# One block layer with two attentions and 32 experts: seven block products in place of eight for half of each gate product's contraction, and experts taken from the four groups in turn

## The chip, the cores and the metric

The kernel runs on one core of one Trainium2 chip. The metric is the device time of one execution in microseconds (us); of several runs the median is given.

## What is computed

One transformer layer over 1024 tokens of width 1024, all in 32-bit floats, then a final norm. Cut to what matters here:

```
h = rmsnorm(x);  proj = h @ w_in            # 4288 columns
qa, ka, va, qi, ki, wi, qb, kvb, gb, gate_a, gate_b = split(proj)   # gate_a, gate_b: 1024 columns each
# branch a: each query keeps the 256 keys with the best index score (qi, ki, wi), then attends to them
score = sum_h wi[h] * relu(qi[h] . ki);  sel = top_k(score, 256)
# branch b: compressed, selected and windowed keys and values, with rope on the keys
merged = sigmoid(gate_a) * (o_a @ w_br_a) + sigmoid(gate_b) * (o_b @ w_br_b)
x = x + merged @ w_out
h = rmsnorm(x)
g = argmax(h @ w_group)                     # one of 4 groups for each token
top-2 of the 8 experts of that group, weighted;  x = x + sum_e w_e * (silu(gate) * up) @ w_down[e]
out = rmsnorm(x)
```

Each token belongs to one group only, so two experts of different groups never hold the same token.

## The kernel before

Every fp32 product runs as three TensorE matmuls: both factors are split into a rounded high part and the rest (h and l), and hh, hl and lh are summed in PSUM. A helper issues the three (the trace names them L238, L239 and L240 of `mm3`). The weights of `w_in` come by DMA as raw chunks of 256 columns; ScalarE (ACT) rounds the high part `wh` (L198) and GpSimd (POOL) subtracts it from the raw one for the low part `wl` (L199). `hTh` and `hTl` are the two parts of the transposed, normed tokens.

The work stands in this order. First the norm and the projections for the compressed branch. Then the query chunks; beside them the "units" of the index: TensorE multiplies the index keys `kist` with the queries (L609), ACT takes the relu (L611), VectorE (DVE) adds the weighted result into the score table `sc` (L615, the last with the row sums `st`). Then the K chunk (columns C_KV+256), 8 token tiles of 24 matmuls 128x256, with rope on POOL (L278 to L281) and transposes and sums into `kB` and `kA` (L667 to L685). Then the gates: 8 chunks (gate_a and gate_b, 2048 columns) of 96 matmuls 128x512, 4 results of 128 columns by 512 tokens each, each followed by a sigmoid on ACT (L860) and a store to `gscr`. Then the V chunk and attention, the merge, and the experts.

Beside the gate chunks DVE looks for each query's 256th best score: 7 rounds (`NCOUNT`) of 6 counts `sc >= th` (L774, widths 384 to 1024), each round but the last followed by some 17 small instructions on 128x6 that narrow the threshold (L781 to L806). Then it writes `okr` (L811), which says whether every query's count was near enough; TensorE transposes it (L813) for the one-row test of a fallback. After that DVE writes the mask `qbias` (L827 to L837).

```
for c in range(8):
    hi, lo = next_chunk()
    for m in range(2):
        for n in range(2):
            ps = ps1.tile([P, 512], F32, name="pj", bufs=2)
            for k in range(KD):
                mm3(ps, hi[:, k, ...m...], lo[:, k, ...m...], hTh[:, k, ...n...], hTl[:, k, ...n...], k == 0, k == KD - 1)
            prefetch()
            ...
            act.activation(gt, ps, AF.Sigmoid)
```

The instructions of the engines are put in an order ahead of the run by a scheduler that knows durations and priorities; each engine then works its list strictly in that order and waits where an operand is not there. So a DVE instruction that is late holds everything behind it on DVE, and a matmul that waits for it holds all matmuls behind it.

The experts run one after the other, 8 of one group and then 8 of the next. For each, weights are streamed and split (`gh`, L1472, `gl`, L1473), tokens are gathered (`xg`, L1453) and transposed (L1463), 96 matmuls make `u` (L238 to L240), silu (L1486, L1495), then `down` (yp, L1504) of the expert before. The weighted result `y` (ACT L1506, DVE L1508) is added to the table `acc` in device memory by an indirect DMA on POOL's queue (`spread`, L1512), each behind the one before. The results of the last two experts stay in SBUF (`keep`, L1625 to L1627, `NL` = 2) and are added to the 8 token tiles of `acc`, read back as `ck` (L1564), by one-hot matmuls (L1643) and a DVE sum (L1644). Then the final norm: L1581 to L1598, and the scaling, on ACT (L1604), POOL (L1583) or DVE (L1608: one instruction 128x1024 with both factors).

Of the kernel before, what the change touches and what calls it, by code (L numbers as in the profile page):

```python
# [20 lines left out]
P = 128  # L21
# [45 lines left out]
ORDER = (2, 3, 7, 6, 5, 1, 4, 0)  # L67

# [33 lines left out]
def emit(tc, A):  # L102
# [107 lines left out]


    chunks = [((C_KV, 256), (C_KI, 32)), ((C_QI, 256), (C_WI, 8), (C_GB, 24))]
# [8 lines left out]
    def prefetch(n=1):  # L221

        if not coming and chunks:
            coming.append(load_chunk(*chunks.pop(0)))
# [70 lines left out]
    def make_list(pl, ps, nm, as_f32=False):  # L295
# [14 lines left out]
        dve.tensor_scalar(i0, f[:, :NXG], -1.0, float(S - 1), op0=OP.add, op1=OP.min)  # L310
# [262 lines left out]
    def index_units(ip):  # L573
# [27 lines left out]
        for t in range(2, NT):  # L601
# [3 lines left out]
            for h in range(8):  # L605
# [11 lines left out]
                if h == 7:  # L617

                    jk = ip.tile([P, 1024], F32, name="jks", bufs=1)
                    act.activation(jk[:, :n], acc, AF.Square, accum_out=st2[:, t - 2:t - 1])  # L620
# [15 lines left out]
    sc = scq.tile([P, 33 * P], F32, name="sc")  # L636
    with ExitStack() as pk:
# [49 lines left out]
        def roped(ps, t):  # L687
            qn = kq.tile([P, 4, 64], F32, name="qn", bufs=4)
            (dve.tensor_copy if t in QND else act.copy)(qn, ps[:, 0:256].rearrange("p (h d) -> p h d", h=4))
            qr = kq.tile([P, 4, 64], F32, name="qr", bufs=4)  # L690
# [3 lines left out]
        def step(t):  # L694
            for _ in range(RATE[t % 2]):
                next(units, None)

        for br, c0 in ((1, C_QB), (0, C_QA)):
            for c in range(2):
                hi, lo = next_chunk()  # L700
                for t in range(NT):
# [10 lines left out]
                    qstack(srcs, t, c)  # L712
        for _ in units:
            pass
        pu.close()

        kp = mkpool(pm, "kp", side="left", reuse_waits="tile")
        kB = [kp.tile([P, 2, 2, S], F32R, name=f"kB{x}") for x in range(2)]
        hi, lo = next_chunk()
        for t in range(NT):  # L720
            ps = project(t, hi, lo, 256)
            _, kr = roped(ps, t)
            if t % 4 == 0:

                ka = kq.tile([P, 4, 64], F32, name="ka")
                cs, sn = (x[:, t:t + 4, None].to_broadcast([P, 4, 2, 32]) for x in (cos, sin))
                ra, rb = (kq.tile([P, 4, 2, 32], F32, name=n, bufs=1) for n in ("ra4_32", "rb4_32"))
                pool.tensor_tensor(ra, kaN[:, t:t + 4], cs, op=OP.mult)
                pool.tensor_tensor(rb, kaN[:, t:t + 4], sn, op=OP.mult)
                kav = ka.rearrange("p t (a b) -> p t a b", a=2)  # L730
                dve.tensor_tensor(kav[:, :, 0], ra[:, :, 0], rb[:, :, 1], op=OP.subtract)
                dve.tensor_tensor(kav[:, :, 1], ra[:, :, 1], rb[:, :, 0], op=OP.add)
            if t % 2:
                late.append(lambda ka=ka, t=t: kapost(ka, t))
            later[1].append(lambda kr=kr, t=t: kpost(kr, t))
        flush()

    with ExitStack() as pk:
        kq = mkpool(pk, "gq", bufs=2, side="left", reuse_waits="tile")
# [5 lines left out]
        with ExitStack() as pt:  # L745
# [93 lines left out]
            with tc.If(fv > 0):  # L839
                for t in range(2, NT):  # L840
# [7 lines left out]
                    dve.tensor_scalar(bias[:, soff[t]:soff[t] + n], y[:, :n], -2.5e38, NEG, op0=OP.is_gt, op1=OP.mult)  # L848

        for c in range(8):  # L850
            hi, lo = next_chunk()
            for m in range(2):
                for n in range(2):
                    ps = ps1.tile([P, 512], F32, name="pj", bufs=2)
                    for k in range(KD):
                        mm3(ps, hi[:, k, m * P:(m + 1) * P], lo[:, k, m * P:(m + 1) * P],
# [881 lines left out]
```

## Time and profile before

| what | value |
|---|---|
| median of 3 runs | 1379.64 us (1377.6 to 1382.06) |
| the profiled execution | 1379.86 us |
| its span | 1378.2 us |
| mean granted TensorE clock | 0.984 |
| busy: PE, DVE, ACT, POOL | 1314.9, 918.9, 699.8, 473.2 us |

Times in the trace count from the start of the span; the profiled execution takes 1.66 us more than its span. PE is TensorE's matmul, DVE VectorE, ACT ScalarE, POOL GpSimd. A row of the timeline gives the start, how long the instruction took, engine, line, what it writes and reads, and in brackets how long the engine stood idle before it and what ended that. Matmuls are pipelined: a row's duration is longer than the distance to the next row, and the distance is what counts.

### The profile page before, as it was taken

The page shows a single profiled execution, that of the slowest core. Times are in us where ns is not written, and L with a number is a line of the kernel's source. Part 1 is how long each engine was busy: PE and PEld are TensorE (multiplying, and loading weights), DVE is VectorE, ACT ScalarE, POOL GpSimd, SP SyncE. Part 2 cuts the span into 40 slices and gives each one's busy share as a digit, 9 for nine tenths or more (in the row PEclk, how much of TensorE's full clock was granted, in tenths as well). Part 3 has the DMA queues.
Part 4 walks back from the last instruction along what each step waited for, and adds up shares of the span by engine and source line. Part 5 has one row for each costly group of instructions (what it writes and reads, how often), then busy time and mean ns, then how long its engine had stood idle before and what let it go on. Part 6 is the DMA issues. An engine that isn't in the chain of part 4 may idle for free. (4 is left out here: it accounts for less than half of the span.)

```text
span 1378.2 us, 21458 instructions
## 1 busy us (share of the span) xinstructions
PE 1314.9 (95%) x7135; PEld 1021.3 (74%) x7135; DVE 918.9 (67%) x2285; ACT 699.8 (51%) x1458; POOL 473.2 (34%) x564
## 2 busy tenths in 40 slices
PE   7999999999999999999999999999699999998993
PEld 6999999988888766666667688877566667665652
DVE  7866877689600588777677686566776767655745
ACT  5615676622211576666676742222366657545544
POOL 0316777722212474444454300000123223223114
PEclk9999999999999999999999999999899999999997
DMA  5513543223333120101110384685799997899866
GB/s 190 124 28 95 158 128 112 70 89 96 93 99 115 31 78 16 31 16 32 46 47 16 107 225 128 205 304 184 240 321 299 323 336 250 260 301 321 298 194 244
DMA packets 127733, 215.34 MB, mean 156 GB/s; under 512 B 24042, under 2 KB 62994, under 8 KB 127618
## 3 DMA queue, kind: packets, MB, share of 16 engines
q1 hardware_dynamic: 111842, 174.53, 38.4%
q0 software_dynamic: 13680, 34.04, 9.2%
q10 hardware_dynamic: 2096, 5.36, 1.0%
q8 instruction: 57, 0.93, 0.3%
q14 instruction: 58, 0.48, 0.1%
HBM read 180.38 MB, written 49.28 MB: 167 GB/s over the span
## 5 line engine op out<-in xcount | busy, mean ns | idle before, releaser
L995 ACT ACTIVATE pg<-pg,nm 128x512 f32<-128x512 f32 (+7 forms) x192 | 139.0, 726 | 49.0 <-DVE nm L994 35.2
L238 PE MATMUL pj<-wh,hTh 128*128 128x288 f32 (+1 forms) x512 | 152.8, 299 | 2.4 <-ACT hTh L421 1.4
L240 PE MATMUL pj<-wh,hTl 128*128 128x288 f32 (+1 forms) x512 | 151.4, 296 | 2.3 <-DVE hTl L422 2.3
L239 PE MATMUL pj<-wl,hTh 128*128 128x288 f32 (+1 forms) x512 | 150.9, 295 | 0.8 <-DVE wl L199 0.8
L199 POOL TENSOR_TENSOR wl<-wr,wh 128x512 fp32r<-128x512 f32 (+1 forms) x60 | 81.5, 1368 | 201.3 <-ACT wh L198 192.2
L1013 PEld LDWEIGHTS tr<-ident,pg 128*128 128x128 f32 x784 | 87.9, 141 | 50.6 <-issue 24.3
L239 PE MATMUL u<-gl,xh 128*128 128x512 f32 x256 | 109.7, 429 | 3.6 <-DVE gl L1473 3.6
L1013 PE MATMUL tr<-ident,pg 128*128 128x128 f32 x784 | 111.1, 277 | 0.0
L238 PE MATMUL u<-gh,xh 128*128 128x512 f32 x256 | 107.2, 419 | 0.7 <-ACT gh L1472 0.7
L240 PE MATMUL u<-gh,xl 128*128 128x512 f32 x256 | 102.2, 399 | 0.0
L238 PE MATMUL pj<-hTh,wh 128*128 128x512 f32 x256 | 101.2, 395 | 0.0
L240 PE MATMUL pj<-hTh,wl 128*128 128x512 f32 x256 | 101.1, 395 | 0.0
L1473 DVE TENSOR_TENSOR gl<-cr,gh 128x1024 fp32r<-128x1024 f32 x68 | 81.7, 1221 | 29.0 <-ACT gh L1472 16.7
L239 PE MATMUL pj<-hTl,wh 128*128 128x512 f32 x256 | 100.8, 394 | 0.0
L1512 POOL DMA_INDIRECT acc<-y,lis x30 | 53.8, 1792 | 136.8 <-ACT y L1506 77.0
L238 PEld LDWEIGHTS pj<-wh,hTh 128*128 128x128 f32 x512 | 97.1, 190 | 4.2 <-ACT hTh L421 2.0
L240 PEld LDWEIGHTS pj<-wh,hTl 128*128 128x128 f32 x512 | 96.8, 189 | 3.8 <-DVE hTl L422 3.1
L239 PEld LDWEIGHTS pj<-wl,hTh 128*128 128x128 f32 x512 | 97.1, 190 | 1.9 <-DVE wl L199 1.0
L916 DVE COPY pth<-tr 128x512 f32<-128x512 f32 (+1 forms) x102 | 69.9, 686 | 38.7 <-PE tr L1013 32.5
L1473 DVE TENSOR_TENSOR gl<-ck,gh 128x1024 fp32r<-128x1024 f32 x55 | 66.6, 1222 | 32.9 <-PE u L239 22.0
L975 PE MATMUL s<-kB,q 128*128 128x384 f32 (+3 forms) x384 | 82.8, 344 | 3.1 <-DVE nm L994 3.0
L916 ACT COPY pth<-tr 128x512 f32<-128x512 f32 (+1 forms) x102 | 58.8, 578 | 46.7 <-PE tr L1013 25.2
(590 smaller groups left out, 3394.5 us busy)
## 6 DMA issues: line engine op xcount, KB each, us to landing
cr<-in_w_gate_up SPq DMA_DIRECT2D x68, 512.0 KB
ck<-in_w_gate_up SPq DMA_DIRECT2D x55, 512.0 KB
cr<-in_w_down SPq DMA_DIRECT2D x32, 512.0 KB
ck<-in_w_down SPq DMA_DIRECT2D x30, 512.0 KB
wr<-in_w_in SPq DMA_DIRECT2D x52, 256.0 KB
qscr<-qTs SPq DMA_DIRECT2D x96, 128.0 KB
q<-qscr POOLq DMA_DIRECT2D x24, 512.0 KB, 3.6
xt<-in_x SPq DMA_DIRECT2D x16, 512.0 KB
```

The lines of the kernel that those rows point to most:

```text
L199: eng.tensor_tensor(lo[:, k:k + 2, w], raw[:, :, w], f32(hi[:, k:k + 2, w]), op=OP.subtract))
L238: pe.matmul(ps, lh, rh, start=first, stop=False)
L239: pe.matmul(ps, lh, rl, start=False, stop=False)
L240: pe.matmul(ps, ll, rh, start=False, stop=last)
L916: return h[:n], (act.copy if EV[ev[0] % len(EV)] else dve.tensor_copy)(h[:n], tr[:n])
L975: mm_, mm = mm, pe.matmul(s2s[x][:, c:c + w_], q()[:, place(h + x)], kk[:, y, j0 * P + c:j0 * P + c + w_], start=y == 0, stop=y == 1)
L995: act.activation(pg, pg, AF.Exp, bias=nm[:, y:y + 1], scale=-1.0, accum_out=sm_[:, y:y + 1])
L1013: pe.transpose(tr[:, hh * P:(hh + 1) * P], pgs[4 * g + hh][:, c:c + P], ident)
L1473: dve.tensor_tensor(gl, w, f32(gh), op=OP.subtract)
L1512: pool.indirect_dma_start(out=acc[:], out_offset=bass.IndirectOffsetOnAxis(ap=idx, axis=0), in_=y, in_offset=None, compute_op=OP.add, boun ...
```

## The change

In each of the gate chunks 1 to 7 (chunk 0 stays as it was) the first half of the contraction, k tiles 0 to 3, is taken as a product of two by two blocks (2 blocks of 128 columns and 2 pairs of k tiles, against 2 pairs of k tiles and 2 blocks of 512 tokens) in seven block products in the place of eight. The second half is done as before. A chunk has 90 matmuls then, not 96. Four of the seven products take sums of token blocks (`sumh`, `suml`, made once in `token_sums`) and three of weight blocks (`sh`, `sl`, made for every chunk by POOL and ACT). The results of several products are shared: they are copied or added in PSUM by ACT (L835, L845) and DVE (L836, L844, L849, L855, L860), five DVE sums of 128x512 in each chunk. The K chunk moves from ahead of the gates to behind them; the transposes for `kA` that went with it move ahead into the last query chunk.

Of the experts one of each group is taken in turn (`EORD`). A spread waits for the fourth before it only, no longer for the three between. The read-back waits for the last four spreads. `keep` of expert 30 runs inside expert 31. In the final norm DVE's scaling reads the gains from PSUM (two matmuls put them there) in two halves.

```diff
+EORD = tuple(8 * g + i for i in range(8) for g in range(4))
...
+    def load_gates(cols):
...
+        def split(h, l, src):
+            act.activation(h, src, AF.Copy)
+            pool.tensor_tensor(l, src, f32(h), op=OP.subtract)
...
+            if k == 2:
...
+                pool.tensor_tensor(f, q[:, :, m[0]], q[:, :, m[1]], op=OP.subtract)
+                split(hi[:, 0:2, m[1]], lo[:, 0:2, m[1]], f)
+                pool.tensor_tensor(f, q[:, :, m[1]], r[:, :, m[1]], op=OP.add)
+                split(sh[:, 0], sl[:, 0], f)
+                pool.tensor_tensor(f, f, q[:, :, m[0]], op=OP.subtract)
+                split(sh[:, 1], sl[:, 1], f)
+                pool.tensor_tensor(f, r[:, :, m[0]], f, op=OP.subtract)
+                split(sh[:, 2], sl[:, 2], f)
...
+    chunks += [((C_GA + 256 * c, 256),) for c in range(8)]
     chunks += [((C_KV + 256, 128), (C_KV + 512, 128))]
-    chunks += [((C_GA + 256 * c, 256),) for c in range(8)]
...
+    def token_sums(pl):
...
+        with tc.high_priority():
+            for k in range(2):
+                for c in range(0, 512, 256):
+                    f = [pl.tile([P, 256], F32, name=f"tf{j}", bufs=1) for j in range(4)]
...
+                        dve.tensor_tensor(f[j], f32(hTh[:, kk + k, at]), f32(hTl[:, kk + k, at]), op=OP.add)
+                    for j, o, x, y in ((0, 0, 1, 0), (1, 1, 2, 1), (2, 2, 2, 0), (3, 3, 3, 2)):
+                        dve.tensor_tensor(f[o], f[x], f[y], op=OP.subtract)
+                        act.activation(th_[:, j, k, cs], f[o], AF.Copy)
+                        dve.tensor_tensor(tl_[:, j, k, cs], f[o], f32(th_[:, j, k, cs]), op=OP.subtract)
...
+            a, b = (ps1.tile([P, 1024], F32, name="s2", bufs=2) for _ in range(2))
+            a, y, z, d = a[:, :512], a[:, 512:], b[:, :512], b[:, 512:]
+            u2, u3 = (kist2[:, j * 512:(j + 1) * 512] for j in range(2))
+            v = ps1.tile([P, 512], F32, name="pj", bufs=2)
+            part(a, w(0, 0), x(0, 0), True, True)
+            part(y, S2, T2, True, True)
+            with tc.high_priority():
+                act.activation(u2, a, AF.Copy)
+                dve.tensor_tensor(u2, y, u2, op=OP.add)
+            part(a, w(2, 0), x(2, 0), False, False)
+            rest(a, 0, 0, False)
+            gate_group(0, 0, a, c)
+            prefetch()
+            part(y, S3, T3, True, True)
+            part(z, S1, T1, True, True)
+            with tc.high_priority():
+                dve.tensor_tensor(u3, y, u2, op=OP.add)
+                act.activation(v, z, AF.Copy)
+            part(d, w(2, 1), T4, True, False)
+            rest(d, 1, 0, False)
+            with tc.high_priority():
+                dve.tensor_tensor(d, d, u3, op=OP.add)
+            gate_group(1, 0, d, c)
+            prefetch()
+            part(z, S4, x(2, 1), False, False)
+            rest(z, 0, 1, False)
+            with tc.high_priority():
+                dve.tensor_tensor(z, z, u2, op=OP.add)
+            gate_group(0, 1, z, c)
+            prefetch()
+            rest(v, 1, 1, False)
+            with tc.high_priority():
+                dve.tensor_tensor(v, v, u3, op=OP.add)
+            gate_group(1, 1, v, c)
+            prefetch()
...
-                        pin(dve.scalar_tensor_tensor(xt, xt, r1, gfin, op0=OP.mult, op1=OP.mult))
+                        for n in range(2):
+                            ns = slice(n * 512, (n + 1) * 512)
+                            pin(dve.scalar_tensor_tensor(xt[:, ns], xt[:, ns], r1, gains[n], op0=OP.mult, op1=OP.mult))
...
-            xts = load_acc()
+            xts = load_acc(spreads[-4:])
...
-                    spread(down(late_[2], dn, lwt[:, col[e]]), lidx[:, col[e]])
+                    i = spread(down(late_[2], dn, lwt[:, col[e]]), lidx[:, col[e]])
+                    if len(spreads) >= 4:
+
+                        for j in spreads[-3:]:
+                            tc.declare_no_dep(i.ins, j.ins, reason="tokens of different groups")
+                        behind(i, spreads[-4], True)
+                    spreads.append(i)
```

`part` issues 6 matmuls (2 k tiles, three each) and `rest` 12. The matmuls of chunks 1 to 7 are all named L807 in the changed kernel, those of chunk 0 L281 to L283, the counts L927, `okr` L964 and its transpose L966.

How the list of TensorE moves at the transpose of `okr`. In the kernel before, all 192 matmuls of the K chunk and 386 of the gates stand ahead of it (`pj` is a gate's result):

```order
L238 MATMUL pj<-hTh,wh 128x512
L239 MATMUL pj<-hTl,wh 128x512
L813 MATMUL tr<-ident,okr 1x128
L240 MATMUL pj<-hTh,wl 128x512
L238 MATMUL pj<-hTh,wh 128x512
```

In the changed one (`s_4745` holds a and y, `s_4746` z and d of chunk 3):

```order
L807 MATMUL s_4745<-hTl,wh 128x512
L807 MATMUL s_4745<-hTh,wl 128x512
L807 MATMUL s_4746<-sumh,wh 128x512
L807 MATMUL s_4746<-suml,wh 128x512
L807 MATMUL s_4746<-sumh,wl 128x512
L966 MATMUL tr<-ident,okr 1x128
L807 MATMUL s_4746<-sumh,wh 128x512
L807 MATMUL s_4746<-suml,wh 128x512
```

Now 315 of the gates' matmuls and none of the K chunk stand ahead of it, and 411 of the gates' behind it.

The list of DVE between the third and the fourth round of counts. Before, only the threshold's small instructions stand there (the first six of them):

```order
L774 TENSOR_SCALAR y,cnt<-sc,th 128x1024
L781 TENSOR_SCALAR mk<-cnt 128x6
L788 TENSOR_SCALAR t_3693<-cnt 128x6
L782 COPY_PREDICATED lo__3688<-mk,th 128x6
L783 COPY_PREDICATED cl<-mk,cnt 128x6
L784 TENSOR_SCALAR mk<-cnt 128x6
```

In the changed kernel three sums of chunk 1 stand among them (`kist` is u3, `s_4456` d, `pj` v):

```order
L927 TENSOR_SCALAR y,cnt<-sc,th 128x1024
L934 TENSOR_SCALAR mk<-cnt 128x6
L941 TENSOR_SCALAR t_3550<-cnt 128x6
L935 COPY_PREDICATED lo__3545<-mk,th 128x6
L936 COPY_PREDICATED cl<-mk,cnt 128x6
L937 TENSOR_SCALAR mk<-cnt 128x6
L938 COPY_PREDICATED hi__3546<-mk,th 128x6
L844 TENSOR_TENSOR kist<-s_4455,kist 128x512
L939 COPY_PREDICATED ch<-mk,cnt 128x6
L849 TENSOR_TENSOR s_4456<-s_4456,kist 128x512
L860 TENSOR_TENSOR pj<-pj,kist 128x512
```

Eleven such sums (five each of chunks 1 and 2, one of chunk 3) stand on DVE between the first count and `okr`, and TensorE's list waits for them: the next block product into the same PSUM tile, or the next chunk's, has one of these sums, or the sigmoid behind it, as its condition. Five more stand among the instructions that write the mask.

On ACT, near the end of the experts, the last of `down` stands behind the silu (`sg`) before, and ahead of it now:

```order
L1486 ACTIVATE sg<-u 128x256
L1506 ACTIVATE y<-yp,lws 128x512
L1472 ACTIVATE gh<-cr 128x1024 x3
L1495 ACTIVATE aT<-at 128x256
L1472 ACTIVATE gh<-cr 128x1024
```

```order
L1662 ACTIVATE y<-yp,lws 128x512
L1628 ACTIVATE gh<-cr 128x1024
L1642 ACTIVATE sg<-u 128x256
L1628 ACTIVATE gh<-cr 128x1024 x2
L1651 ACTIVATE aT<-at 128x256
```

Both pieces stand near the end of the expert stage. TensorE's `down` moves with it, ahead of the last 5 matmuls of the expert that runs beside it.

## Rows read from the trace of the kernel before

**Rows 1.** Page, busy time and share of the span by engine, instructions.

```profile
PE 1314.9 (95%) x7135; PEld 1021.3 (74%) x7135; DVE 918.9 (67%) x2285; ACT 699.8 (51%) x1458; POOL 473.2 (34%) x564
```

**Rows 2.** Windows: busy us (instructions) of PE, PEld, DVE, ACT, POOL, clock, DMA share.

```profile
300.00:350.00 50.00, 50.00 (x218) 40.44 (x217) 47.30 (x163) 9.95 (x19) 10.35 (x9) 1.00 0.29 90
...
400.00:450.00 50.00, 50.00 (x265) 42.68 (x264) 0.85 (x2) 7.90 (x15) 9.88 (x10) 1.00 0.35 106
```

**Rows 3.** Timeline of PE: first K matmul, okr's transpose, V's first matmul.

```profile
231.91 0.36 PE L238 MATMUL pj<-wh,hTh 128*128 128x256 f32 x1
...
349.70 0.27 PE L813 MATMUL tr<-ident,okr 128*1 128x128 f32 x1
...
438.36 0.28 PE L238 MATMUL pj<-wh,hTh 128*128 128x256 f32 x1
```

**Rows 4.** Timeline of DVE: last scores, starts of rounds 1 to 3, okr, mask's end.

```profile
248.10 1.28 DVE L615 SCALAR_TENSOR_TENSOR sc<-s,raw,sc 128x1024 f32<-128x1024 f32 x1 [0.50 <-ACT s L611]
...
284.67 0.61 DVE L774 TENSOR_SCALAR_CACHE_REDUCE y<-sc,th 128x384 bf16<-128x384 f32 x1
...
293.16 0.61 DVE L774 TENSOR_SCALAR_CACHE_REDUCE y<-sc,th 128x384 bf16<-128x384 f32 x1
...
301.04 0.61 DVE L774 TENSOR_SCALAR_CACHE_REDUCE y<-sc,th 128x384 bf16<-128x384 f32 x1
...
343.71 0.14 DVE L811 TENSOR_REDUCE okr<-mk 128x1 f32<-128x6 f32 x1
...
367.34 1.22 DVE L837 TENSOR_SCALAR qbias<-y 128x896 bf16<-128x896 f32 x2
```

**Rows 5.** Groups of DVE by shape, 231 to 281 us: the work on kA.

```profile
L684 DVE SCALAR_TENSOR_TENSOR kA<-tr,kA 64x128 fp32r<-64x128 f32 x8 | 2.3, 288 | 4.2 <-ACT kA L682 4.1
L685 DVE CAST kA<-kA 64x256 fp32r<-64x256 f32 x4 | 1.8, 442 | 0.1
```

**Rows 6.** Timeline of DVE: sums of two SBUF operands, 341 to 343 us.

```profile
341.83 0.55 DVE L828 TENSOR_TENSOR y<-y,sc 128x384 f32<-128x384 f32 x1
342.30 0.15 DVE L809 SCALAR_TENSOR_TENSOR mk<-cnt,t 128x6 f32<-128x6 f32 x1
...
342.64 0.68 DVE L828 TENSOR_TENSOR y<-y,sc 128x512 f32<-128x512 f32 x1
```

**Rows 7.** Timeline: a small DVE instruction of the search, and POOL beside it.

```profile
283.28 1.27 DVE L794 TENSOR_TENSOR t<-sd,tkc 128x6 f32<-128x6 f32 x1
...
283.22 2.58 POOL L199 TENSOR_TENSOR wl<-wr,wh 128x512 fp32r<-128x512 f32 x2 [4.61 <-ACT wh L198]
```

**Rows 8.** Chain that ended last, pieces in time order: start, us, what.

```profile
1346.07 0.70 DVE ck L1644
...
1361.90 3.14 DVE ck L1608
...
1366.35 1.28 DVE ck L1608
```

**Rows 9.** Timeline of ACT: the sigmoid of a gate result.

```profile
271.76 0.60 ACT L860 ACTIVATE gt<-pj 128x512 f32<-128x512 f32 x1
```

**Rows 10.** Waits of PE, 1290 to 1345 us: total, times, longest.

```profile
PE yp L1504 <- ACT y L1506: 1.1, 1, 1.1
PE yp L1625 <- ACT y L1506: 1.1, 1, 1.1
```

**Rows 11.** Timeline: the last two spreads, the last y, the last kept result.

```profile
1329.61 1.56 POOL L1512 DMA_INDIRECT acc<-y,lis  x1 [8.52 <-DVE gl L1473]
1336.42 1.56 POOL L1512 DMA_INDIRECT acc<-y,lis  x1 [5.25 <-DVE ck L1627]
...
1332.15 0.68 ACT L1506 ACTIVATE y<-yp,lws 128x512 f32<-128x512 f32 x1
...
1342.39 0.75 DVE L1627 SCALAR_TENSOR_TENSOR ck<-yp,lws,ck 128x512 fp32r<-128x512 f32 x1 [0.97 <-ACT ck L1626]
```

**Rows 12.** Windows, 24 to 32 us (columns as in Rows 2).

```profile
24.00:32.00 8.00, 6.28 (x28) 5.30 (x28) 7.48 (x20) 5.45 (x15) 0.00 (x0) 0.59 0.23 67
```

More of the change, by code (lines that the diff above doesn't have):

```diff
@@ L715, in emit @@
         pu.close()
[L717 to L735, printed above, removed]
@@ L736, in emit, with gate_group, part @@
-        flush()
-    with ExitStack() as pk:
-        kq = mkpool(pk, "gq", bufs=2, side="left", reuse_waits="tile")
+        pg0 = ExitStack()
+        gq.append(mkpool(pg0, "g0", bufs=2, side="left", reuse_waits="tile"))
+        def gate_group(m, n, ps, c):
+            gt = gq[0].tile([P, 512], F32, name="gt")
+            act.activation(gt, ps, AF.Sigmoid)
+            sp.dma_start(gscr[2 * c + m, :, n * 512:(n + 1) * 512], gt)
+        def part(ps, a, b, first, last):
+            (ah, al), (bh, bl) = a, b
+            for k in range(2):
+                for x, y in ((ah, bh), (ah, bl), (al, bh)):
+                    pe.matmul(ps, x[:, k], y[:, k], start=first and k == 0 and y is bh and x is ah,
+                              stop=last and k == 1 and x is al, skip_group_check=True)
@@ new lines, in emit, with first_gates @@
+        token_sums(gq[0])
+        first_ = next_chunk()
+        def first_gates(m):
+            hi, lo = first_
+            for n in range(2):
+                ps = ps1.tile([P, 512], F32, name="pj", bufs=2)
+                for k in range(KD):
+                    mm3(ps, hi[:, k, m * P:(m + 1) * P], lo[:, k, m * P:(m + 1) * P],
+                        hTh[:, k, n * 512:(n + 1) * 512], hTl[:, k, n * 512:(n + 1) * 512], k == 0, k == KD - 1)
+                if m:
+                    prefetch(2)
+                gate_group(m, n, ps, 0)
+                if not m:
+                    todo = later[0] + late
+                    later[:] = later[1], []
+                    late.clear()
+                    for f_ in todo:
+                        f_()
@@ L742, in emit @@
+        first_gates(0)
+        pg0.close()
+    pg_ = ExitStack()
+    gq[:] = [mkpool(pg_, "gq", bufs=2, side="left", reuse_waits="tile")]
+    first_gates(1)
+    with pg_:
         bias = small.tile([P, 33 * P], BF, name="qbias")
@@ L871, in emit @@
     flush()
+    pk.close()
     p1.close()
@@ L1569, in final @@
             pin = tc.keep_in_program_order
+            gains = [gfin[:, n * 512:(n + 1) * 512] for n in range(2)]
             s1s, q1s, z1s, r1s = {}, {}, {}, {}
@@ L1578, in sums @@
                 if add:
-                    add(t, xts[t])
+                    i = add(t, xts[t])
+                    if t == 3:
+                        for n in range(2):
+                            gp = psf.tile([P, 512], F32, name="yp", bufs=2)
+                            behind(pe.matmul(gp, ident, gains[n], start=True, stop=True), i)
+                            gains[n] = gp
                 jk = ft.tile([P, D], F32, name="y", bufs=NY)
@@ L1686, in between @@
                 turn_next(e + 1)
+            elif c >= 2 and e + 1 == NE:
+                keep((c - 2,))
         for c in range(4):
```

123 lines of the change are left out of this document (92 added, 31 removed).

## The prediction

> **What bounds the kernel now.** I read the page first: TensorE is busy for 1314.9 of 1378.2 us [rows 1], so it idles for 63 us in all, and what moves the time is what shortens or delays its own list. The windows come next [rows 2]. From 300 to 350 us PE is busy for every microsecond at clock 1.00, with 217 matmuls of 128x512 (0.23 us each), and VectorE has 47.30 us of work; from 400 to 450 PE is as full and DVE has 0.85. DVE is thus nearly full beside the first half of the gates and idle beside the second, and this costs nothing today, for one reason: the only matmul that waits for the counting is the transpose of `okr`, issued at 349.70 [rows 3], and DVE writes `okr` from 343.71 on [rows 4]. The slack is nearly 6 us. The end of the kernel is the other place without cover: there the chain that ended last runs from a spread over the read-back to DVE's sums and scaling.
>
> **The change part by part.**
>
> *Products.* Seven chunks with 90 matmuls in place of 96 are 42 fewer; 50.00 us hold 217 [rows 2], so 0.23 each: −9.7 us of PE.
>
> *The K chunk behind the gates.* Its 192 matmuls cost PE the same there. What goes is cover. Today PE starts it at 231.91 and reaches `okr`'s transpose 117.8 us later [rows 3]. In the changed list 315 gate matmuls, 14 index matmuls and 11 small transposes stand between the same point and that transpose: 329 × 0.23 = 75.7, and 11 × 0.15 = 1.7 (an estimate: a row of such a transpose reads 0.27, and rows overlap). PE would be there at 309.3, 40 us sooner.
>
> *DVE until `okr`.* Today the last scores end at 249.4, counting starts at 284.67, and `okr` is there at 343.85 [rows 4], 59.2 us later. Changed:
> - The work on `kA` now stands ahead of the last scores: 8 × 0.288 + 4 × 0.442 = 4.1 us [rows 5]. The scores end at 253.5.
> - 48 token sums of 128x256. No row has that size with two SBUF operands; 384 took 0.55 and 512 took 0.68 [rows 6], so 256 takes about 0.42; the next row starts 0.08 before an end (341.83 and 0.55, then 342.30): 48 × 0.34 = 16.3. The search's 22 preparing instructions lie between: 2.5 at 0.11 each, an estimate below the 0.15 that such a row takes [rows 6]. Counting starts at 272.3.
> - From the first count to `okr` 59.2, as today. Six rounds of 7.88 when undisturbed (293.16 to 301.04 [rows 4]) are 47.3, and the last one's counts and the tail about 8.1 (an estimate: 17 small instructions fewer than a round's 7.88 leave 5.2, and 2.9 go to the tail), so 3.8 of it are delays. They are small instructions beside a POOL one: 1.27 in place of 0.15, until the first half of POOL's 2.58 was over [rows 7]. POOL's work for a chunk goes from 2048 elements a partition to 3840, nearly double: 3.8 more.
> - 11 gate sums of 128x512. The nearest row, one operand in PSUM, took 0.70 [rows 8], some 0.60 from start to start: 6.6.
>
> Sum: 272.3 + 59.2 + 3.8 + 6.6 = 341.9. **TensorE waits about 33 us in place of none**, and not in one piece. Its first wait is for the token sums: chunk 1's z stands behind 102 gate matmuls, so PE is there near 261, while the sums end near 272 and ACT and POOL still have to split `sh`. The others are for the sums u2 and u3 and for sigmoids behind z, each of which has a round of counts in front of it.
>
> The Trainium skill's page "SBUF — State Buffer" (section "SBUF: two separate sides") says that GpSimd and a VectorE instruction with two SBUF inputs lock each other out for a whole instruction. Rows 7 agree, with 1.27 us. By that rule the 48 token sums too would stand in line with whatever POOL does beside them, which makes the sum above longer, not shorter.
>
> *After `okr`.* DVE writes the mask, 343.85 to 368.5 today, 24.7 us [rows 4], with five gate sums (3.0) among it; the last of these lets PE go on, 69 matmuls (15.9 us) behind the transpose: 27.7 − 15.9 = 11.8, less the two mask writes behind that sum (1.2): 10 us. Then DVE is free from 400 us on [rows 2], and a chain is left at three chunk ends: product, DVE sum 0.70, sigmoid 0.60, next chunk's product into the same PSUM tile [rows 8, 9]: 1.3 and the handovers, 5 in all.
>
> Gates and K together: −9.7 + 33 + 10 + 5 = **+38 us**. Bounds: if the scores end as today and no instruction is delayed at all, the wait is 33 − 4.1 − 7.6 = 21 and the total +26; if a sum of two PSUM operands, which no row has, takes a pass for each, 11 × 0.6 more, +45. I take the middle: the sum with one PSUM operand is the nearest row.
>
> The Trainium skill's page "VectorE: DVE Perf Modes" (section "Why PSUM operands drop a tier") states that VectorE has one read port to PSUM. An estimate by it would be two passes for such a sum; no row here shows one.
>
> *Copies, weight sums, DMA.* ACT has 9.95 and POOL 10.35 us of work in 50 [rows 2]: two copies a chunk on the one and twice the work on the other hide there, and the bytes are the same. Zero.
>
> *Experts and end.* Bytes and matmuls of the 32 experts stay. Two waits of PE for ACT's `y`, 1.1 each [rows 10], go, since `y` stands ahead of the silu. The last spread is issued at 1336.42, 6.8 behind the one before, though its `y` was ready at 1332.83 [rows 11]; unhooked, it lands some 4 us sooner. Next in line is the last kept result, ready at 1343.14 [rows 11], and two waits sooner at 1341: so the first sum moves from 1346.07 [rows 8] to about 1341.2, −4.9. L1608 of 3.14 us becomes two halves of the undisturbed 1.28 [rows 8]: −1.8. Two fp32 matmuls for the gains: +0.9 at most. **−6 us**; bounds −2 (landings side by side stretch each other) and −9.
>
> **Sum:** 1379.9 + 38 − 6 = 1412 us; the profiled run lies 0.2 above the median, so this stands against that as well. A change below 0.3% (4 us) can't be told from none by a measurement of this kernel.
>
> **Rivals.**
> - *Light tie, 1400 us.* The scores end as today and nothing is delayed: 1379.9 + 26 − 6. For it: whole rounds have no late row (293.16 to 301.04). Against it: POOL's longer work. 0.16.
> - *The other side, 1364 us.* DVE answers every gate sum before PE asks, because the sums have priority over the counts: 1379.9 − 9.7 − 6. It decides at the transpose of `okr`: DVE has to be there by 309, and by about 315 for the whole kernel to break even (6 us of wait, 10 behind it). Rounds and tail alone are 55.4, so counting would have to begin near 254, which leaves no room for the token sums. Against it: the list has them in front. 0.07.
> - *Heavy tie, 1425 us.* PSUM sums cost double (+7), and the gaps cost clock: between short idle times early on, 6.28 of 8.00 us busy, the granted clock was 0.59, near the 1.2 GHz level [rows 12]; a gate matmul at that level takes 0.23 more, and 25 of them are +6. For it: the 43 us of waiting come in several pieces. Against it: while DVE is the bound, a slow PE is partly hidden. 0.15.
> - *The expert part gives nothing,* 1418: a case inside the forecast's range.
>
> **How the numbers follow.** The forecast has 0.62, the light tie 0.16, the heavy one 0.15, the other side 0.07. The range leaves out the other side and the outer parts of the two ties: 1394 to 1431. Slower by over 0.3%: 0.90; faster: 0.07; within 0.3%: 0.03, as little lies between the light tie and the other side.
>
> **What would show it.** In the profile after: PE idle for some 45 us between 260 and 440, released by DVE L844 and L836 and by ACT's sigmoid; `okr` near 342 and its transpose right behind; V's first matmul near 476 in place of 438.36 [rows 3]; 128x512 sums of about 0.7; the first sum of the tail right behind the last kept result. I would be wrong if `okr` came before 325, if PE had no long waits ahead of it, or if the gate sums were far from 0.7.

## The result and the profile after

The changed kernel takes 1429.68 us (median of 4 runs, 1427.22 to 1431.28) against 1378.95 us for the kernel before (4 runs): ratio 1.0356, 95% interval 1.0333 to 1.038. It is slower by 50.7 us. The forecast was 1412 us with a range of 1394 to 1431: the direction and the range held, the range by 1.3 us at its upper end, and the middle lay 17.7 us too low.

The page of the changed kernel, engine by engine: busy time, share of the span, instructions. The next line is the granted clock of TensorE in 40 slices.

```profile
PE 1332.3 (93%) x7097; PEld 1028.5 (72%) x7097; DVE 967.4 (68%) x2370; ACT 721.3 (50%) x1516; POOL 509.7 (36%) x620
...
PEclk8999999799899999999999999999979999999998
```

Against [rows 1] PE has 38 matmuls fewer (42 fewer in the gates, 4 more for the gains of the final norm) and is busy 17.4 us longer, and the span grew by 51.3 us. So PE both waits more and is slower while it works. The windows of the gate stage of the changed kernel show both (columns as in [rows 2]: busy us of PE, PEld, DVE, ACT and POOL with their instructions, clock, DMA share, GB/s):

```profile
260.00:300.00 40.00, 25.06 (x93) 18.89 (x91) 39.21 (x125) 14.00 (x31) 18.07 (x22) 0.83 0.23 66
300.00:350.00 50.00, 40.85 (x154) 31.87 (x155) 47.58 (x146) 12.89 (x27) 19.27 (x23) 0.90 0.24 74
350.00:400.00 50.00, 40.35 (x149) 30.86 (x147) 27.18 (x50) 8.97 (x20) 13.91 (x16) 0.86 0.21 64
400.00:450.00 50.00, 44.62 (x183) 35.42 (x184) 7.74 (x12) 15.19 (x32) 21.73 (x25) 0.96 0.28 85
```

From 300 to 350 us PE was full at clock 1.00 before [rows 2]; now it is busy 40.85 of 50 us and starts 154 matmuls and transposes where it started 218. The granted clock is 0.83 to 0.90 as long as DVE is busy with the search and the mask, and even from 400 on, where DVE has 7.74 us of work in 50, PE is not full.

Where PE waited in the changed kernel, from 225 to 500 us (who waits, for whom: us in total, times, longest); it is the view's whole answer:

```profile
PE s L807 <- ACT gt L799: 18.1, 7, 5.0
PE s L807 <- DVE kist L844: 10.3, 3, 5.2
PE s L807 <- ACT sh L225: 9.1, 1, 9.1
PE s L807 <- DVE kist L836: 1.6, 1, 1.6
PE s L807 <- DVE sc L658: 1.3, 1, 1.3
PE s L652 <- DVE sc L658: 1.3, 2, 0.9
PE tr L741 <- DVE qTs L721: 0.9, 2, 0.6
```

`gt` is the sigmoid (ACT), `kist` the sums u2 and u3 (DVE), `sh` the rounded weight sums. The kernel before has no such wait in its gates.

**Where 51.3 us of span come from.** I cut each span at two places that both kernels have: attention's first matmul (461.19 us before, 516.43 after) and the transpose of the experts' first gathered tokens (1001.65 and 1057.63). Up to attention the change adds 55.2 us, between the two places 0.7, and behind the second it saves 4.6 (376.51 to 371.91). The 55.2 are, by the list of PE's starts: 42 matmuls fewer, −9.7; 47.1 in 23 gaps (a gap is here and below a step of over 0.5 us from the start of a 128x512 matmul to the next start, less 0.23); 77 matmuls of 128x512 that are some 0.43 us from the next in place of 0.23, +14.9; the rest, some 3, was not followed further. Of the 23 gaps 15 are waits, 44.3 us. The other 8, 2.9 us, are no idle time: they are the first steps behind a wait where the granted clock was already at 0.50, 0.56 to 0.59 us in place of the 0.34 that such a step takes at 1.00. So the lower clock makes 14.9 + 2.9 = 17.8 us, and the waits 44.3.

### The profile page after: what moved, and what is told of

It is laid out like the page before. It is cut to its first block, busy times and chain, and to the rows that moved or that the text cites. A ratio compares the mean times of both kernels' runs of the same rounds, so it can differ in the third digit from the quotient of the medians.

```text
span 1429.5 us, 21637 instructions
## 1 busy us (share of the span) xinstructions
PE 1332.3 (93%) x7097; PEld 1028.5 (72%) x7097; DVE 967.4 (68%) x2370; ACT 721.3 (50%) x1516; POOL 509.7 (36%) x620
## 4 chain that ended last, share of the span: by engine, by line
PE 78%; DVE 11%; DMA 4%; ACT 3%; issue 3%; DVEq 0%; POOL 0%; ACTq 0%; POOLq 0%
PE av L1079 7%; PE yp L1660 7%; PE s L1131 7%; PE tr L1169 7%; PE s L807 6%; PE pj L283 4%; PE pj L281 4%; PE pj L282 4%; PE ps L281 4%; PE u L282 4%; PE ps L283 4%; PE ps L282 4%; PE u L281 4%; PE u L283 3%; DVE y L927 2%
## 5 line engine op out<-in xcount | busy, mean ns | idle before, releaser
L283 PE MATMUL pj<-wh,hTl 128*128 128x288 f32 (+1 forms) x512 | 152.0, 297 | 2.7 <-DVE hTl L465 2.7
L281 PE MATMUL pj<-wh,hTh 128*128 128x288 f32 (+1 forms) x512 | 152.9, 299 | 1.6 <-ACT hTh L464 1.4
L1668 POOL DMA_INDIRECT acc<-y,lis x30 | 51.3, 1709 | 186.7 <-ACT y L1662 161.7
L282 PE MATMUL u<-gl,xh 128*128 128x512 f32 x256 | 113.4, 443 | 1.8 <-DVE gl L1629 1.5
L281 PE MATMUL u<-gh,xh 128*128 128x512 f32 x256 | 105.5, 412 | 3.1 <-ACT gh L1628 3.1
L283 PE MATMUL u<-gh,xl 128*128 128x512 f32 x256 | 102.1, 399 | 0.0
L283 PEld LDWEIGHTS pj<-wh,hTl 128*128 128x128 f32 x512 | 97.2, 190 | 3.8 <-DVE hTl L465 3.5
L281 PEld LDWEIGHTS pj<-wh,hTh 128*128 128x128 f32 x512 | 97.6, 191 | 2.9 <-ACT hTh L464 1.8
L1629 DVE TENSOR_TENSOR gl<-ck,gh 128x1024 fp32r<-128x1024 f32 x55 | 66.8, 1225 | 37.0 <-PE u L282 17.7
L1628 ACT ACTIVATE gh<-cr 128x1024 fp32r<-128x1024 f32 x68 | 70.7, 1058 | 34.4 <-DMA cr<-in_w_gate_up 26.4
L201 POOL TENSOR_TENSOR wl<-wr,wh 128x576 fp32r<-128x576 f32 (+1 forms) x32 | 44.8, 1408 | 108.7 <-ACT wh L200 99.2
L1150 DVE CUSTOM_DVE_ANT_0 pg<-s,causal 128x256 f32<-128x256 f32 (+7 forms) x112 | 65.0, 616 | 7.6 <-PE s L1131 7.2
L1628 ACT ACTIVATE gh<-ck 128x1024 fp32r<-128x1024 f32 x55 | 58.2, 1060 | 23.2 <-DMA ck<-in_w_gate_up 11.0
```

Of the source, the lines that this page charges most:

```text
L281: pe.matmul(ps, lh, rh, start=first, stop=False)
L282: pe.matmul(ps, lh, rl, start=False, stop=False)
L283: pe.matmul(ps, ll, rh, start=False, stop=last)
L1628: act.activation(gh, w, AF.Copy)
L1629: dve.tensor_tensor(gl, w, f32(gh), op=OP.subtract)
```

## The experiments

Eight kernels, each timed beside the kernel before. Their ratios are to that kernel on the same chip.

### One part alone: the experts and the end

The front is as before, with K ahead of the gates and eight products everywhere; the turns of the groups, the spreads, `keep` inside expert 31 and the new end stay.

Edit, against the kernel before:

```diff
+EORD = tuple(8 * g + i for i in range(8) for g in range(4))
...
+                    if len(spreads) >= 4:
+
+                        for j in spreads[-3:]:
+                            tc.declare_no_dep(i.ins, j.ins, reason="tokens of different groups")
+                        behind(i, spreads[-4], True)
...
-            xts = load_acc()
+            xts = load_acc(spreads[-4:])
```

> The kernel before with the second part of the change alone: experts of the four groups in turn, spreads that wait for the fourth before, keep split, gains of the final norm in PSUM; gates and K chunk as before. My theory: this part is worth what the trace of the changed kernel shows from the first transposed token of the experts to the end of the span, 371.9 us against 376.6: about -4.7, so 1374 us (1372 to 1377), and V's first matmul stays near 438. Rival: the expert part shares in the loss (its spreads side by side slow the weight streams), the gates lose less than 55: then this one is no faster than before, 1379 or more.

Measured: 1373.88 us against 1380.86, ratio 0.9945 (0.9927 to 0.9963). The stretch from the experts' first transpose to the end is 371.0 us, 5.5 shorter than before, and the attention starts at 462.04, 0.9 later than before. So this part gains, the whole loss is in the front, and **this kernel beats both**: by 0.55% against the kernel before, and the interval leaves 1 out.

### All eight products, K still behind the gates

Edit, against the changed kernel:

```diff
-            coming.append(load_gates(cols) if C_GA < cols[0][0] < C_END else load_chunk(cols, eng))
+            coming.append(load_gates(cols) if C_GA + 256 * 8 <= cols[0][0] < C_END else load_chunk(cols, eng))
...
-        token_sums(gq[0])
...
+                    for k in range(KD):
+                        mm3(ps, hi[:, k, m * P:(m + 1) * P], lo[:, k, m * P:(m + 1) * P],
+                            hTh[:, k, n * 512:(n + 1) * 512], hTl[:, k, n * 512:(n + 1) * 512], k == 0, k == KD - 1)
```

> The changed kernel with eight products in every gate chunk, as before; the K chunk stays behind the gates, the experts in turn. My theory: the loss of 55 us ahead of attention is that of the seven-product scheme in chunks 1 to 7 (waits of 47 us, 77 matmuls at half clock), and the moved K chunk costs next to nothing: 1374 to 1379 us, no wait of PE over 3 us between 260 and 440, okr near 320 with its transpose when PE gets there. Rival: the moved K chunk, which takes away PE's cover of 27 us, makes PE wait at okr whatever the gates do: 1390 us or more.

Measured: 1383.03 us against 1380.86, ratio 1.001 (0.9995 to 1.0026), above what I expected. The attention starts at 468.52, 6.5 later than in the kernel above, from which it differs by K's place and what moved with it (the transposes for `kA` and the sizes of a few buffers). Its waits in the gate stage, in the same view:

```profile
PE pj L281 <- ACT gt L800: 2.4, 1, 2.4
PE s L652 <- DVE sc L658: 1.3, 2, 0.9
PE tr L742 <- DVE qTs L722: 0.9, 2, 0.6
```

All three lie near 245 to 252 us, where the last query chunk's index units end. In the kernel before, K's matmuls (231.91 to 258.85) stand at this place and cover them; 10 half-rate matmuls behind them add 2. `okr` is there at 316.83 and nothing waits for it. So with eight products the move of K costs about 6.5 us, through small waits at the seam and not through `okr`. Seven products with K still ahead of the gates were not run; what K's place costs together with them is open.

### DVE set free

The search rounds and the mask's making are left out (the counts and the mask are constants); all else of the change stays.

Edit, against the changed kernel:

```diff
-            for it in range(NCOUNT):
-                count()
...
+            dve.memset(cnt, TOPK - 2.0)
...
+            dve.memset(bias, 0.0)
```

> The changed kernel with the search left out: no rounds of counts, and the mask of the 256 best keys is a constant zero. Token sums, gate sums and all matmuls stay. My theory as on record (DVE's counts stand in front of the gate sums) says that the waits ahead of okr and beside the mask go, and what is left is the wait for the token sums (about 11 us) and a chain at the end of each chunk, DVE sum and sigmoid into the next chunk's tile (2.4 us each at six or seven ends): some 28 us in place of 47, fewer matmuls at half clock, 1398 to 1406 us. Rival: the seven-product scheme has these waits from its own chain of copies, sums and sigmoids in few PSUM tiles, whatever else DVE does: 1420 us or more. If DVE's counts were all there is: 1375 us.

Measured: 1407.37 us against 1380.86, ratio 1.0187 (1.0157 to 1.0218), a little above what I expected. The attention starts at 493.01, 23.4 us sooner than in the changed kernel; 41 matmuls are at half rate and 25.3 us go in gaps. So DVE's load is a little under half of the loss, and the seven products lose even where DVE has almost nothing to do. The waits that are left, in the same view (the longest two of eight lines):

```profile
PE s L807 <- ACT gt L799: 12.4, 6, 2.1
PE tr L937 <- issue: 6.2, 1, 6.2
```

The first is one wait of 2.1 us in almost every chunk. One of them, on PE and then on DVE and ACT of the same kernel (start, duration, engine, instruction, in brackets the idle time before and what ended it):

```profile
329.04 0.40 PE L807 MATMUL s<-hTh,wl 128*128 128x512 f32 x1
331.51 0.50 PE L807 MATMUL s<-sumh,sh 128*128 128x512 f32 x1 [2.07 <-ACT gt L799]
```

```profile
329.55 0.70 DVE L855 TENSOR_TENSOR s<-s,kist 128x512 f32<-128x512 f32 x1 [6.35 <-PE s L807]
```

```profile
329.24 0.94 ACT L225 ACTIVATE wh<-wr 128x256 fp32r<-128x256 f32 x2 [6.42 <-PE s L807]
330.08 0.40 ACT L225 ACTIVATE wh<-sf 128x256 fp32r<-128x256 f32 x1
330.39 0.58 ACT L835 ACTIVATE kist<-s 128x512 f32<-128x512 f32 x1
330.87 0.59 ACT L799 ACTIVATE gt<-s 128x512 f32<-128x512 f32 x1
```

PE ends `z`; DVE adds u2 to it (L855); the sigmoid stands in ACT's list behind three roundings and a copy and ends at 331.46; and the very next matmul of PE's list is the next chunk's product into the tile that `z` was in. A chunk saves 6 matmuls, 6 × 0.23 = 1.4 us, and this wait takes 2.1.

### DVE free, and five PSUM tiles

In the change `a` and `y` are the halves of one PSUM tile of 128x1024, `z` and `d` of another. Here each has a tile of its own. Search and mask are left out as above.

Edit, against the kernel with DVE free:

```diff
-            a, b = (ps1.tile([P, 1024], F32, name="s2", bufs=2) for _ in range(2))
-            a, y, z, d = a[:, :512], a[:, 512:], b[:, :512], b[:, 512:]
+            z, d = (ps1.tile([P, 1024], F32, name="s2", bufs=2)[:, :512] for _ in range(2))
+            a = ps1.tile([P, 512], F32, name="pj", bufs=2)
+            y = ps1.tile([P, 512], F32, name="tr", bufs=2)
```

> The run without search and mask, and the five partial results a, y, z, d and v of a chunk in five PSUM tiles of their own, where the changed kernel keeps a and y in one tile and z and d in another. My theory: the 2.4 us at the chunk ends come from these shared tiles (a write into one half waits for the readers of the other, which forces TensorE's list into an order that puts the next chunk's z right behind this one's); with five tiles they go, and with them the half-clock matmuls behind them: 17 us of waits and 8 to 10 us of clock less than the run without search, 1373 to 1380 us. Rival: the chain of product, DVE sum and sigmoid is the limit in itself: within 4 us of the run without search.

Measured: 1385.68 us against 1380.86, ratio 1.0035 (1.0017 to 1.0053); above what I expected. The attention starts at 469.35, 23.7 us sooner than with the shared tiles. Two of the five lines of the same view:

```profile
PE tr L938 <- issue: 7.1, 1, 7.1
PE pj L281 <- ACT gt L799: 1.8, 1, 1.8
```

No wait at a chunk's end is left, and from 300 to 400 us PE is busy for all 100 us at clock 1.00. PE's list shows why: with shared tiles the 18 matmuls that end `z` stand right ahead of the next chunk's product into the same pair; with five tiles the 12 of `v`, 6 of `a` and 6 of `y` stand between, 24 × 0.23 = 5.5 us, and the sum and the sigmoid are done by then. Against the kernel with the experts alone (462.04) there are left the seam at K and 7.1 us in which the transpose of `okr` waits for DVE, which makes the token sums until then (`okr` at 272.99), with 20 slow matmuls in all, less the 9.7 of the fewer products: 6.5 + 7.1 + 2.0 for ten slow ones more − 9.7 = 5.9 of the 7.3 us between the two. Five tiles with the search and the mask in place were not run.

### DVE free, gaps filled with useless matmuls

As the first kernel with DVE free, plus 98 matmuls of 128x512 whose result nobody reads: 28 ahead of `okr`'s transpose and 10 ahead of `z`'s first product in each of seven chunks.

Edit, against the kernel with DVE free:

```diff
+            spare = spares(10, ends[-1])
+            i0 = part(z, S1, T1, True, True)[0]
+            for i in spare:
+                behind(i0, i)
...
+            l = spares(28, ends[-1])
```

> The run without search and mask (1407.4 us; gates and K chunk 258.9 us from the first gate matmul to attention, 41 matmuls at half clock), with 98 useless matmuls of 128x512 into a spare PSUM tile: 28 in the wait ahead of okr's transpose and 10 in the wait at the head of each of the chunks 1 to 7. They add 22.5 us of TensorE work and take no wait away. My theory: the half-clock matmuls come from the idle time in front of them; with the gaps filled fewer than 15 are left, and the kernel is 5 to 7 us faster although it does more, 1400 to 1403 us. Rival: the clock falls with the kind of work or at random, or the useless matmuls get in the way: 1407 us or more.

Measured: 1399.49 us against 1381.9, ratio 1.0119 (1.0096 to 1.0142), against 1.0187 (1.0157 to 1.0218) without them: 98 × 0.23 = 22.5 us of matmuls more, and the kernel is faster by 0.7%, a little more than I expected. Half-rate matmuls fall from 41 to 12, and 29 × 0.2 = 5.8 us is about the 5.5 by which the stage from the first gate matmul to attention gets shorter. The same window of the two, without and then with the useless matmuls (columns as above):

```profile
300.00:350.00 50.00, 45.82 (x189) 36.27 (x189) 6.96 (x10) 13.71 (x29) 22.46 (x26) 0.97 0.33 100
```

```profile
300.00:350.00 50.00, 50.00 (x216) 40.24 (x216) 7.73 (x12) 15.41 (x33) 22.37 (x27) 1.00 0.29 89
```

PE has no idle time in this window, and the clock stays at 1.00. The waits are filled here, not shortened: gaps fall by 20.4 us, a wait of 2.3 right behind `okr`'s transpose goes too, and the useless matmuls take 22.5. So the slow matmuls come from the gaps, and here, where DVE is free, they are a cost on top of them.

### Without the token sums

The products read the plain token blocks in place of `sumh` and `suml`; the 48 DVE sums and 16 ACT roundings are left out. Search and mask are there.

Edit, against the changed kernel:

```diff
-            T1, T3, T2, T4 = ((th_[:, j], tl_[:, j]) for j in range(4))
+            T1, T3, T2, T4 = ((hTh[:, 2 * (j // 2):2 * (j // 2) + 2, n[j % 2]], hTl[:, 2 * (j // 2):2 * (j // 2) + 2, n[j % 2]]) for j in range(4))
...
-        token_sums(gq[0])
```

> The changed kernel with the token sums left out: the seven products take plain token blocks in their place, so the gates are not the reference's; the same 90 matmuls a chunk, the same gate sums, counts and mask. My theory: DVE's list is 16 to 20 us shorter in front of the counts, okr comes near 332 in place of 345.7, and TensorE, which hangs on DVE until then, gains 11 to 16 us: 1414 to 1420 us. Rival: the token sums hide beside chunk 0 and only the counts matter, or the chain at the chunk ends takes the place: 1425 us or more.

Measured: 1415.34 us against 1381.9, ratio 1.025 (1.0226 to 1.0274); as expected. The stage from the first gate matmul to attention is 15.1 us shorter than in the changed kernel: 11.1 less in gaps and 23 half-rate matmuls fewer. Its two longest waits:

```profile
PE s L807 <- DVE kist L844: 14.0, 3, 5.2
PE s L807 <- ACT gt L799: 12.3, 6, 2.1
```

The wait for `sh` (9.1) is gone, while that for u3 is longer (14.0 against 10.3): the gate sums still stand among the search.

### The experts, with each spread behind the one before

Edit, against the kernel with the experts alone:

```diff
-                    if len(spreads) >= 4:
-
-                        for j in spreads[-3:]:
-                            tc.declare_no_dep(i.ins, j.ins, reason="tokens of different groups")
-                        behind(i, spreads[-4], True)
```

> The expert part alone, as in the run of 1373.9 us, but each spread again behind the one before, as in the kernel before. My theory: the last spread then lands about 3 us later and the read-back with it, and the rest (y ahead of the silu, gains in PSUM) stays: 1376 to 1378 us. Rival: the moved y is all that counts, spreads being 11 us apart and landing in under 10: 1373 to 1375 us, no difference.

Measured: 1379.31 us against 1381.9, ratio 0.9984 (0.9969 to 0.9998), a little above what I expected. From the experts' first transpose to the end it takes 375.72 us, against 371.0 with the spreads side by side and 376.51 in the kernel before. The last spread and its wait, with the spreads side by side and then in series (POOL's timeline):

```profile
1326.14 1.55 POOL L1514 DMA_INDIRECT acc<-y,lis  x1 [7.88 <-ACT y L1508]
```

```profile
1338.71 1.56 POOL L1514 DMA_INDIRECT acc<-y,lis  x1 [5.16 <-DVE ck L1642]
```

In series the two waits of PE for `y` of [rows 10] are back at 1.1 us each: the scheduler puts `y` behind the silu again. Of the 5.5 us that the experts gain, 4.7 come with the spreads side by side. Two things make them: the last kept result ends 340.9 us behind the experts' first transpose in place of 342.6, where `y` stands ahead of the silu again, and the first sum of the tail starts right behind that result, where in series it starts 2.9 later, after the last spread has landed. The turns, `keep` and the new end give 0.8 without the spreads; as this stretch took 369.5 to 373.1 us in the seven other kernels with the new end and the spreads side by side, 0.8 can't be told from none.

### Seven products in the last two chunks only

Eight products in chunks 0 to 5, seven in 6 and 7, with five PSUM tiles and the token sums behind `okr`, where DVE is free; K behind the gates. The result is the full computation.

Edit, against the kernel with all eight products:

```diff
-        for c in range(1, 8):
+        for c in range(1, 6):
...
+            token_sums(kt)
```

> The run with eight products in every chunk and the K chunk behind the gates (1383.0 us beside 1380.9 of before), with seven products in chunks 6 and 7 only, where DVE is done with the mask; token sums behind okr, five partial results in five PSUM tiles. My theory: with nothing on DVE in front of the gate sums and no shared tiles, the saving of 6 matmuls a chunk is real: 2 x 1.38 = 2.8 us less than the run with eight products everywhere, no wait of PE over 1 us in the chunks 6 and 7. Rival: sums, copies and sigmoids cost more than 6 matmuls even there: the same or more.

Measured: 1382.27 us against 1381.9, ratio 1.0008 (0.9992 to 1.0023). In the trace the stage from the first gate matmul to attention takes 235.13 us against 237.93 with eight products throughout: −2.80, which is twice 6 × 0.23. So the saving is there in the trace, as expected, to the amount of the matmuls, where both covers are there. In the run's time it can't be told from none, and it does not pay for the move of K.

## Why the prediction was right, and what it mis-sized

**Products, −9.7.** Held: the kernel with seven products in two chunks gains 1.40 a chunk in the trace, where 6 × 0.23 = 1.38 was the term.

**DVE until `okr`.** The forecast was 341.9; the trace of the changed kernel has 345.70 (DVE's timeline: the last token sum ahead of the first count, that count, three gate sums among the search's small instructions, `okr`):

```profile
271.01 0.42 DVE L695 TENSOR_TENSOR tf<-tf,tf 128x256 f32<-128x256 f32 x1
271.34 0.61 DVE L927 TENSOR_SCALAR_CACHE_REDUCE y<-sc,th 128x384 bf16<-128x384 f32 x1
...
299.56 0.69 DVE L844 TENSOR_TENSOR kist<-s,kist 128x512 f32<-128x512 f32 x1
300.16 0.44 DVE L939 COPY_PREDICATED ch<-mk,cnt 128x6 f32<-128x6 int32 x1
300.52 0.69 DVE L849 TENSOR_TENSOR s<-s,kist 128x512 f32<-128x512 f32 x1
301.12 0.68 DVE L860 TENSOR_TENSOR pj<-pj,kist 128x512 f32<-128x512 f32 x1
...
345.70 0.13 DVE L964 TENSOR_REDUCE okr<-mk 128x1 f32<-128x6 f32 x1
```

The count starts at 271.34 (272.3 forecast). A token sum takes 0.42 and the next instruction starts 0.33 to 0.34 behind it, both as worked out from the sizes 384 and 512 of [rows 6], and a gate sum 0.69, 0.6 from start to start. From the first count to `okr` it is 74.4, not 69.6. Of the difference of 4.8, 1.3 is DVE's own wait for a product and 0.7 are two token sums behind the first count. The rest is mostly small instructions beside POOL: from the first count to `okr` 20 of the 104 on 128x6 took over 0.25 us, each beside a POOL instruction and ending within 0.04 us of its end, 9.9 us more in all than 0.17 each; in the kernel before there are 5 of them, 4.0 us. So POOL's double work added 5.9 us, where 3.8 were forecast. L939 above took 0.44, in place of 0.17 as most of its kind. POOL's timeline at the same time:

```profile
299.85 0.72 POOL L243 TENSOR_TENSOR sf<-wr 128x256 f32<-128x256 f32 x1 [0.99 <-DMA wr<-in_w_in]
```

It ends at 300.57, and L939 at 300.60; the gate sum L844, which reads PSUM, overlaps the same instruction and keeps its 0.69. This is the delay of [rows 7] again, and POOL's double work was rightly given a price, if too low a one. These rows agree with the rule cited from the Trainium skill's page "SBUF — State Buffer" (section "SBUF: two separate sides"). The token sums, against my reading of it, kept their pace, as POOL stood idle beside most of them (below).

**Sums of two PSUM operands.** The bound of +7 was for sums of two PSUM operands. There is no such sum in the kernel: u2 and u3 lie in SBUF, so each gate sum reads one operand from PSUM and takes 0.69. I misread where u2 and u3 lie, and the bound had no ground. The rule that stood beside it, of the Trainium skill's page "VectorE: DVE Perf Modes" (section "Why PSUM operands drop a tier"), has no bearing on such a sum: 0.69 is what two SBUF operands take as well (0.68, [rows 6]). No run shows two PSUM operands.

**PE's waits, 33 + 10 + 5 = 48.** Held in size: 44.3 in 15 waits. By place: 28.0 up to `okr`'s transpose (with 2.7 at the seam at 245 to 252, which I had not counted), 9.7 beside the mask and 6.6 at the last three chunk ends. That the first term is below 33 goes with the lower clock: PE came to these waits later than forecast (below). The first long one is on the way that was forecast, with one more step. PE's timeline, and then POOL's and ACT's (same columns):

```profile
265.75 0.40 PE L283 MATMUL pj<-hTh,wl 128*128 128x512 f32 x1
275.26 0.79 PE L807 MATMUL s<-sumh,sh 128*128 128x512 f32 x1 [9.12 <-ACT sh L225]
```

```profile
256.32 0.91 POOL L243 TENSOR_TENSOR sf<-wr 128x256 f32<-128x256 f32 x1
273.23 0.72 POOL L226 TENSOR_TENSOR wl<-sf,wh 128x256 fp32r<-128x256 f32 x1 [16.01 <-ACT wh L225]
```

```profile
271.46 0.42 ACT L696 ACTIVATE sumh<-tf 128x256 fp32r<-128x256 f32 x1 [0.33 <-DVE tf L695]
271.78 1.06 ACT L799 ACTIVATE gt<-pj 128x512 f32<-128x512 f32 x2
272.74 0.42 ACT L225 ACTIVATE wh<-sf 128x256 fp32r<-128x256 f32 x1
274.79 0.42 ACT L225 ACTIVATE sh<-sf 128x256 fp32r<-128x256 f32 x1 [1.64 <-POOL sf L245]
```

POOL had the first difference of weights ready at 257.2, but its rounding stands on ACT behind all 16 roundings of token sums, each of which waits for DVE. So the token sums hold ACT, ACT holds POOL for 16 us, and PE waits 9.12. The kernel without token sums has no wait for `sh`.

**Chunk ends, 5 in all: the size held, the reason only in part.** I had product, DVE sum, sigmoid, next product into the same tile. The rows above show that, with three roundings and a copy ahead of the sigmoid, and the place in PE's list decides: the kernel with five tiles has none of these waits. I had taken the wait as part of seven products; it belongs to the two shared tiles. With DVE free it stands at six chunk ends, and this is why freeing DVE alone does not save the change.

**The clock: the step that failed.** The forecast's sum has no term for it; the heavy rival had "25 of them are +6". The runs show 77 matmuls at half rate and 8 slow first steps, +17.8, in the forecast's own case. V's first matmul, forecast near 476, came at 492.97, 17 us later. By the trace 3.8 of these 17 are DVE, which wrote `okr` later than forecast. Another 2.9 are PE, which came to `okr`'s transpose at 348.60 without a wait, when `okr` had been there since 345.8. The other 10.3 are lost behind the transpose, and 8.1 of them are slow matmuls. PE's timeline of the changed kernel at a chunk end (the rows between are alike):

```profile
401.34 0.50 PE L807 MATMUL s<-sumh,sh 128*128 128x512 f32 x1 [2.06 <-ACT gt L799]
...
402.17 0.63 PE L807 MATMUL s<-sumh,sh 128*128 128x512 f32 x1
402.60 0.63 PE L807 MATMUL s<-suml,sh 128*128 128x512 f32 x1
...
405.55 0.40 PE L807 MATMUL s<-hTh,wl 128*128 128x512 f32 x1
```

From 402.17 on the distance is 0.43 in place of 0.23, and the granted clock of 402.2 to 405.4 us reads 0.50: this is the lower of the two levels, 1.2 GHz. Eight matmuls later it is back. A gap of 2.06 us thus costs 3.7. The kernel with filled gaps shows that the gaps are the cause. The argument against the clock in the prediction, that a slow PE is partly hidden while DVE is the bound, held only ahead of `okr`: there the lower clock takes 9.7 us, and PE is 2.9 late at the transpose. Behind it the 8.1 came on top, and no term stood for them. This is worked out from the one trace; a kernel with filled gaps and the search in place was not run.

**Experts and end, −6.** The stretch behind the experts' first transpose got 4.6 us shorter. The scaling: one pair of 1.41 a tile in place of 3.14 and 1.28 of [rows 8], −1.6 on two tiles (−1.8 + 0.9 forecast). The first sum of the tail stands right behind the last kept result, as forecast (DVE's timeline):

```profile
1398.70 0.75 DVE L1796 SCALAR_TENSOR_TENSOR ck<-yp,lws,ck 128x512 fp32r<-128x512 f32 x1 [0.97 <-ACT ck L1795]
1399.37 0.68 DVE L1813 TENSOR_TENSOR ck<-u,ck 128x512 f32<-128x512 f32 x1
...
1417.78 1.41 DVE L1775 SCALAR_TENSOR_TENSOR ck<-ck,rs_q,yp 128x512 f32<-128x512 f32 x2
```

Counted from the experts' first transpose it starts at 341.7 in place of 344.4: −2.7, not −4.9. The step that fell is "two waits sooner at 1341": the last kept result ends 341.8 behind that transpose, as before (341.5), though the two waits of [rows 10] are gone. What took back their 2.2 us was not tried; four shorter ones, of 1.2 us together, stand there now.

**The range, and the rivals.** With the terms above the forecast's way explains the time, but that the range held is owed in part to luck: its upper end was taken from the heavy tie, not from the sum, it held by 1.3 us, and the profiled run of 1431.28 lies just outside. The other side, 1364 us, needed `okr` by 309; it came at 345.70. The light tie, 1400, needed no delays; there are more than I put in. The heavy tie, 1425, is nearest in time, and one of its two reasons is right: the clock, with 17.8 us of slow matmuls in place of 6.

## What to carry to other kernels

Fewer matmuls help only where the engines that must answer between them (here DVE for a sum, ACT for a rounding and a sigmoid) have room and other matmuls stand between the question and the answer; count both for each chunk, 1.4 us saved against 2.1 us of wait. When a wait is put into a full stretch of TensorE, add the slow matmuls behind it to the sum from the start: here 17.8 us beside 44.3 of waits. Where TensorE then waits for another engine, part of them is hidden (ahead of `okr` here); where it is itself the bound, they count in full. A PSUM tile that two results share ties the first product of the next turn to the last reader of this one: look where the next product into that tile stands in the list, and give it a tile of its own before working on the reader.

## What had not been expected of the hardware

- The lower level of TensorE's clock came after gaps of some 2 us in a stretch that was full otherwise. The same gap was not always followed by it: at 401.34 of the changed kernel 2.06 us idle were followed by eight slow matmuls, and at 331.51 of the kernel with DVE free 2.07 us by none (331.85 to 332.08 is 0.23 already). What tells the two apart was not found.
- Work that nobody needs made a kernel faster: 98 matmuls, 22.5 us of TensorE's time, and the ratio falls from 1.0187 to 1.0119.
